# A two-layer decoder trunk on one core: a fixed TensorE order, another head grouping in layer A, and a softmax per token tile in layer B

## The chip, the cores and the metric

The kernel runs on one core of a Trainium2 chip. The metric is the device time of one execution in microseconds, the median of several runs. TensorE (PE in the profile) multiplies matrices; VectorE (DVE), ScalarE (ACT) and GpSimd (POOL) do the elementwise work, each taking its own queue in order; SyncE (SP) issues the DMAs.

## What is computed

A residual stream x of 256 tokens by 1024 goes through two layers in float32. Layer A is causal differential attention with 8 heads, each with two query/key pairs of width 64 and one value of width 128. Layer B is causal dilated sliding-window attention with 16 heads in each of three dilation groups. Each attention is followed by a squared-ReLU MLP of width 4096. Cut to what matters here:

```python
# layer A, per head h, components c = 0, 1
q, k, v = split(rms_norm(x, a_norm) @ w_qkv)       # q, k: RMS norm per 64, gain, rotary
p = softmax(mask(q @ k.T * 64 ** -0.5))            # for c = 0 and c = 1
o = (p[0] - lam * p[1]) @ v
x = x + rms_norm(o, sub_gain) * (1 - lam_init) @ w_o
x = x + square(relu(rms_norm(x) @ w_up)) @ w_down
# layer B: own q, shared k and v, groups (window, dilation) = (128,1), (512,4), (2048,16)
# per-head outputs of the groups are mixed by their softmax denominators: one softmax over all groups' keys
x = x + mix(softmax(mask(q @ k.T * 64 ** -0.5)) @ v) @ w_o
x = x + square(relu(rms_norm(x) @ w_up)) @ w_down
```

## The kernel before

Every float32 matrix product is made of three reduced-precision products: each operand is split into a high and a low part (high*high, high*low, low*high). For weights the class `Weights` does this: a chunk comes by DMA into one of three `raw` buffers (`fetch`, L69), ScalarE rounds half a chunk to `whi` (L82), VectorE subtracts to get `wlo` (L83); there are five buffers of each half. `W.pump` (L96) splits up to four halves ahead of the one in use.

Tokens lie in two tiles of 128 (t = 0, 1). `gemm` (L297) makes a projection of 384 columns in four weight halves; `gemm_half` (L283) issues 12 matmuls per half (2 token tiles x 2 contraction tiles x 3 products). After each half stands a call of `tick` (L211). In layer A a projection is one head: 128 columns of q, 128 of k, 128 of v. In layer B it is q, k or v of one head pair in all three groups, so three projections make one pair.

`qk_rows` (L310) turns the projected q and k of a token tile into normed, rotated rows: a square on ScalarE (L315), a multiplication by the rotary table on VectorE (`T`, L317), a sum (L321) and a scaling (L323) there, and three GpSimd operations (L328, L332, L334).

The attention of a head (or pair) is a Python generator, `attn_A` (L522) or `attn_B` (L596), whose stages are separated by `yield`; a yield of n is resumed n ticks later. The waits stand in `WAIT_A` and `WAIT_B` (L40, L41). The stages in layer A: transposes of q and k (`qk_T`, L352); scores (L350) with mask and row maximum on VectorE (`masked`, L368), then the negated and scaled maximum `nm` (L538), four exponentials on ScalarE (L541), and the combination of the two softmaxes (L545 to L550); transposes of the probabilities (L554); products with v (L565, L566) and the norm of the output (L569 to L580); transposes of the output (L584) and its split into `oh`, `ol`. In layer B: `qk_T` three times; scores of token tile 0 and 1 with their masks (L609); then one softmax stage over both tiles (L612 to L623: `nm`, exponentials, reciprocal, scaling); per head of the pair transposes (L632) and products with v (L646); at the end the split into `oh`, `ol` (L652).

PSUM has 8 banks in one ring (tag "bank"). A projection takes two, the output projection (`OutProj`, L390) four until its end, `qk_T` one, a pair of scores two, a group of transposes or products one.

After the last projection the output projection runs for heads 0 to 5, with a tick after each half of a head, and `finish` (L227) ticks until the head in question is done; the last two heads are added in `boundary` (L372) together with the start of the next stage. The instructions of each engine are put in order at compile time by a scheduler that goes by priorities and its own estimate of times; TensorE's too.

```python
WAIT_A = (2, 2, 4, 2, 3)
WAIT_B = (2, 2, 2, 2, 2, 3)
    for kt in range(KT - 2):
        finish(gens[kt])
        op.body(kt)
    for kt in range(KT - 2, KT):
        finish(gens[kt])
```

## Time and profile before

| what | value |
|---|---|
| median of 3 runs | 802.08 us (801.34 to 802.3) |
| the profiled execution | 801.55 us, its span 799.5 us |
| TensorE busy | 772.1 us (97%), 4408 matmuls |
| VectorE busy | 581.1 us (73%) |
| ScalarE busy | 467.0 us (58%) |
| GpSimd busy | 190.9 us (24%) |
| mean granted TensorE clock | 0.995 |
| layer A, first projection to first MLP matmul | 10.64 to 137.12 us |
| MLP of layer A | 137.12 to 317.65 us |
| layer B, first projection to first MLP matmul | 317.65 to 616.68 us |
| MLP of layer B | 616.68 us to the end |

Matmuls are pipelined, so a row's duration is longer than the time until the next may start; the distance between the starts of neighbouring rows is what one costs in a stream. The idle time in brackets at a row's end is counted from the modelled end of the matmul before it, so it is a little shorter than the time that was lost.

### The profile page before, as it was taken

What the parts mean: (1) busy time and instruction counts of PE and PEld (TensorE: products, weight loads), DVE (VectorE), ACT (ScalarE), POOL (GpSimd) and SP (SyncE); (2) the same over time, 40 slices, a digit from 0 to 9 for tenths busy, and PEclk for the clock granted to TensorE, in tenths of its full rate; (3) what the DMA queues carried; (4) which work ended last, traced back from release to release, by engine and by line L of the source; (5) the groups of instructions that cost most, each with busy time, mean ns of one, the idle gap of its engine ahead of it and who ended that gap; (6) DMA issues with size and microseconds to landing.
All of it is one profiled execution on the core that took longest, in us unless ns stands there. A gap on an engine that the chain in (4) does not pass through costs nothing.

```text
span 799.5 us, 11766 instructions
## 1 busy us (share of the span) xinstructions
PE 772.1 (97%) x4408; PEld 686.7 (86%) x4408; DVE 581.1 (73%) x985; ACT 467.0 (58%) x851; POOL 190.9 (24%) x191
## 2 busy tenths in 40 slices
PE   6999989999999999999999999999997999999998
PEld 6898967888888888999999999999886888888886
DVE  3998987666656666998888888888767666556663
ACT  5667777544444445657586674857766544444441
POOL 2553531300000000555336354363611000000000
PEclk9999999999999999999999999999999999999999
DMA  8643445445555542554443434434442455545531
GB/s 300 229 143 123 158 155 164 169 171 197 198 176 207 171 184 90 187 198 154 136 153 113 157 121 157 158 119 172 159 158 106 158 186 182 210 170 199 187 130 52
DMA packets 22328, 131.12 MB, mean 164 GB/s; under 512 B 2560, under 2 KB 3328, under 8 KB 13056
## 3 DMA queue, kind: packets, MB, share of 16 engines
q1 hardware_dynamic: 22272, 130.38, 46.0%
q8 instruction: 34, 0.56, 0.3%
q14 instruction: 22, 0.18, 0.1%
HBM read 129.32 MB, written 1.05 MB: 163 GB/s over the span
## 4 chain that ended last, share of the span: by engine, by line
PE 64%; DVE 17%; ACT 12%; issue 3%; POOL 2%; DMA 1%; SPq 0%; POOLq 0%; DVEq 0%; ACTq 0%
PE wps L435 15%; PE wps L437 7%; PE acc L488 7%; PE acc L489 7%; PE acc L490 7%; DVE wlo L83 5%; PE acc L292 4%; PE acc L294 4%; PE acc L293 4%; ACT whi L82 4%; ACT sm L618 2%; DVE sm L369 2%; PE wps L632 2%; DVE T L317 2%; ACT smA L541 2%
## 5 line engine op out<-in xcount | busy, mean ns | idle before, releaser
L83 DVE TENSOR_TENSOR wlo<-raw,whi 128x1024 fp32r<-128x1024 f32 (+1 forms) x272 | 307.0, 1138 | 153.9 <-ACT whi L82 153.7
L82 ACT ACTIVATE whi<-raw 128x1024 fp32r<-128x1024 f32 (+1 forms) x272 | 258.9, 957 | 211.1 <-issue 74.9
L435 PE MATMUL wps<-hT,whi 128*128 128x512 f32 x512 | 182.2, 399 | 2.0 <-DVE hT L271 2.0
L437 PE MATMUL wps<-hT,wlo 128*128 128x256 f32 x512 | 142.9, 280 | 0.0
L435 PEld LDWEIGHTS wps<-hT,whi 128*128 128x128 f32 x512 | 95.9, 188 | 26.0 <-DVE hT L271 3.2
L328 POOL TENSOR_TENSOR T<-T 128x384 f32<-128x384 f32 (+1 forms) x48 | 44.4, 924 | 280.5 <-DVE ms L243 181.6
L488 PE MATMUL acc<-whi,u 128*128 128x512 f32 x256 | 100.4, 392 | 0.3 <-ACT u L340 0.3
L489 PE MATMUL acc<-wlo,u 128*128 128x512 f32 x256 | 100.0, 391 | 0.0
L490 PE MATMUL acc<-whi,u 128*128 128x512 f32 x256 | 98.9, 389 | 0.0
L437 PEld LDWEIGHTS wps<-hT,wlo 128*128 128x128 f32 x512 | 96.6, 189 | 1.4
L292 PE MATMUL acc<-whi,hT 128*128 128x384 f32 x256 | 88.8, 349 | 0.3 <-ACT whi L82 0.2
L292 PE MATMUL acc<-whi,hK 128*128 128x384 f32 x256 | 87.6, 343 | 0.0
L293 PE MATMUL acc<-wlo,hT 128*128 128x384 f32 x256 | 86.3, 337 | 1.1 <-DVE wlo L83 1.1
L294 PE MATMUL acc<-whi,hT 128*128 128x384 f32 x256 | 86.2, 337 | 0.0
L294 PE MATMUL acc<-whi,hK 128*128 128x384 f32 x256 | 85.8, 335 | 0.0
L293 PE MATMUL acc<-wlo,hK 128*128 128x384 f32 x256 | 85.7, 335 | 0.0
L332 POOL TENSOR_TENSOR f<-ms,half 128x6 f32<-128x6 f32 (+1 forms) x48 | 68.2, 1422 | 4.6 <-DVE ms L323 3.1
L488 PEld LDWEIGHTS acc<-whi,u 128*128 128x128 f32 x256 | 48.1, 188 | 11.7 <-ACT u L340 1.2
L490 PEld LDWEIGHTS acc<-whi,u 128*128 128x128 f32 x256 | 48.1, 188 | 10.6 <-DVE u L341 0.4
L489 PEld LDWEIGHTS acc<-wlo,u 128*128 128x128 f32 x256 | 48.1, 188 | 8.8
L293 PEld LDWEIGHTS acc<-wlo,hT 128*128 128x128 f32 x256 | 48.6, 190 | 1.4 <-DVE wlo L83 1.4
L292 PEld LDWEIGHTS acc<-whi,hT 128*128 128x128 f32 x256 | 48.6, 190 | 1.4 <-ACT whi L82 0.5
(117 smaller groups left out, 1204.9 us busy)
## 6 DMA issues: line engine op xcount, KB each, us to landing
raw<-in_wB SPq DMA_DIRECT2D x48, 768.0 KB, 4.2
raw<-in_wup SPq DMA_DIRECT2D x32, 1024.0 KB, 4.8
raw<-in_wdn SPq DMA_DIRECT2D x32, 1024.0 KB, 4.8
raw<-in_wA SPq DMA_DIRECT2D x15, 768.0 KB, 4.3
raw<-in_woA SPq DMA_DIRECT2D x4, 1024.0 KB, 4.8
raw<-in_woB SPq DMA_DIRECT2D x4, 1024.0 KB, 4.8
early<-in_x SPq DMA_DIRECT2D x2, 512.0 KB, 5.3
x<-in_xp SPq DMA_DIRECT2D x1, 1024.0 KB, 7.5
```

Of the source, the lines that this page charges most:

```text
L82: self.nc.scalar.activation(hi[:, :n], raw, AF.Copy)
L83: self.nc.vector.tensor_tensor(lo[:, :n], raw, hi[:, :n].bitcast(F32), op=ALU.subtract)
L292: nc.tensor.matmul(ps, h[:, kt, 0, tok], wh[:, c], start=kt == 0, stop=False)
L293: nc.tensor.matmul(ps, h[:, kt, 0, tok], wl[:, c], start=False, stop=False)
L294: nc.tensor.matmul(ps, h[:, kt, 1, tok], wh[:, c], start=False, stop=kt == KT - 1)
L328: nc.gpsimd.tensor_tensor(u[:, :n].rearrange("p (h a d) -> p h a d", a=2, d=HD // 2), T[:, 0, :n].rearrange("p (h a d) -> p h a d", a=2, d ...
L332: nc.gpsimd.tensor_tensor(f[:, :nsub], ms[:, :nsub], half[:, :nsub], op=ALU.pow)
L435: nc.tensor.matmul(o, wh[:, c], self.h[:, kt].rearrange("p l s -> p (l s)"), start=kt == 0, stop=False, skip_group_check=True)
L437: nc.tensor.matmul(o[:, 0:S], wl[:, c], self.h[:, kt, 0, :], start=False, stop=kt == KT - 1, skip_group_check=True)
L488: nc.tensor.matmul(ps, uh[:, tok], dh[:, c], start=first, stop=False)
L489: nc.tensor.matmul(ps, uh[:, tok], dl[:, c], start=False, stop=False)
L490: nc.tensor.matmul(ps, ul[:, tok], dh[:, c], start=False, stop=last)
```

## The change

TensorE's instructions keep the order of the source: `tc.manual_schedule` takes that engine away from the scheduler. The other engines' orders are still made by it.

Layer A's projections are regrouped. A "qk" unit projects q and k of two heads (512 columns, four weight halves of two contraction tiles), a "v" unit the values of two heads (256 columns, two weight halves of four contraction tiles), in the order `UNITS`. A tick now also stands between the two token tiles of a half. The waits `WAIT_A` are longer in ticks, and the odd head of a unit waits three more. `qk_rows` handles both heads at once up to L332 and writes the product `T` into a part of the buffer `early`.

In both layers `masked` yields the negated, scaled minimum `nm` directly, with the scores scaled along, so the separate `nm` operation is gone. In layer A two more small VectorE operations go: one to ScalarE (a square), one to GpSimd (an addition of 128x2). In layer B the softmax is made per token tile, right after that tile's scores, and the projections of the last two pairs are reordered (`PAIRS`); a pair's attention starts after its k projection, with a longer wait.

```diff
-WAIT_A = (2, 2, 4, 2, 3)
-WAIT_B = (2, 2, 2, 2, 2, 3)
+WAIT_A = (7, 3, 6, 3, 5)
+WAIT_B = (4, 2, 2, 5, 2, 3)
+UNITS = [("qk", 0), ("qk", 1), ("v", 0), ("qk", 2), ("v", 1), ("qk", 3), ("v", 2), ("v", 3)]
+PAIRS = [(hp, i) for hp in range(HP - 2) for i in range(3)]
+PAIRS += [(HP - 2 + e, i) for e, i in ((0, 0), (0, 1), (1, 0), (1, 1), (0, 2), (1, 2))]
...
+    def gemm_A(h, key, n, nk):
+        pss = [accum() for _ in range(NT)]
+        for half in range(KT // nk):
+            gemm_half(pss, h, key, half // 2, half % 2, n, nk, tick)
+            if half < KT // nk - 1:
+                tick()
+        return pss
...
-        qn = wk.tile([P, 384], F32, name="qn", tag="qn", bufs=6)
-        nc.gpsimd.tensor_tensor(
-            qn[:, :n].rearrange("p (h d) -> p h d", d=HD), u[:, :n].rearrange("p (h d) -> p h d", d=HD),
-            f[:, :nsub, None].to_broadcast([P, nsub, HD]), op=ALU.mult)
+        for e in range(heads):
+            qn = wk.tile([P, 384], F32, name="qn", tag="qn", bufs=6)
+            nc.gpsimd.tensor_tensor(
+                qn[:, :n].rearrange("p (h d) -> p h d", d=HD),
+                u[:, e * n:(e + 1) * n].rearrange("p (h d) -> p h d", d=HD),
+                f[:, e * nsub:(e + 1) * nsub, None].to_broadcast([P, nsub, HD]), op=ALU.mult)
+            rows.append(qn)
...
-    def masked(out, ps, m, init, mx):
-        nc.vector.tensor_tensor_reduce(out, ps, m, 1.0, init, ALU.add, ALU.max, mx)
+    def masked(out, ps, m, nm):
+        nc.vector.tensor_tensor_reduce(out, ps, m, -(HD ** -0.5), 3e38, ALU.add, ALU.min, nm)
...
-        yield WAIT_A[0]
+        yield WAIT_A[0] + 3 * (hd % 2)
...
-        nm = small.tile([P, 4], F32, name="nm", tag="nm")
-        nc.vector.tensor_scalar(nm, mx, -(HD ** -0.5), None, op0=ALU.mult)
...
-        nc.vector.scalar_tensor_tensor(cf[:, :, 1], den[:, :, 0], EPS, den[:, :, 0], op0=ALU.mult, op1=ALU.mult)
+        nc.scalar.activation(cf[:, :, 1], den[:, :, 0], AF.Square, scale=EPS ** 0.5)
...
-        nc.vector.scalar_tensor_tensor(ms[:, :2], oss, 1.0 / P, cf[:, :, 1], op0=ALU.mult, op1=ALU.add)
+        nc.gpsimd.tensor_tensor(ms[:, :2], oss, cf[:, :, 1], op=ALU.add)
...
+            nm = small.tile([P, 2], F32, name="nm", tag="nm")
             for hh in range(2):
                 masked(sms[hh][:, b, :], scs[hh], mask[:, 4 * b:4 * b + 4, :].rearrange("p b k -> p (b k)"),
-                       -3e38, mxs[hh][:, b:b + 1])
-            yield WAIT_B[2 + b]
-        for hh in range(2):
-            sm = sms[hh]
+                       nm[:, hh:hh + 1])
             den = small.tile([P, 2], F32, name="den", tag="den")
-            nm = small.tile([P, 2], F32, name="nm", tag="nm")
-            nc.vector.tensor_scalar(nm, mxs[hh], -(HD ** -0.5), None, op0=ALU.mult)
-            for b in range(2):
-                nc.scalar.activation(sm[:, b, :], sm[:, b, :], AF.Exp, bias=nm[:, b:b + 1], scale=HD ** -0.5,
-                                     accum_out=den[:, b:b + 1])
+            for hh in range(2):
+                nc.scalar.activation(sms[hh][:, b, :], sms[hh][:, b, :], AF.Exp, bias=nm[:, hh:hh + 1],
+                                     scale=-1.0, accum_out=den[:, hh:hh + 1])
             rd = small.tile([P, 2], F32, name="rd", tag="rd")
             nc.vector.reciprocal(rd, den)
-            for b in range(2):
-                nc.scalar.activation(sm[:, b, :], sm[:, b, :], AF.Copy, scale=rd[:, b:b + 1])
-        yield WAIT_B[2]
+            for hh in range(2):
+                nc.scalar.activation(sms[hh][:, b, :], sms[hh][:, b, :], AF.Copy, scale=rd[:, hh:hh + 1])
+            yield WAIT_B[2 + b]
...
+    for kind, u in UNITS:
+        if kind == "qk":
+            pss = gemm_A(h, ("qk", u), 512, 2)
...
+            for t in range(NT):
+                tab = tabA[:, t].rearrange("p c g d -> p c (g d)")[:, :, None, :].to_broadcast([P, 2, 2, 4 * HD])
+                rows.append(qk_rows(pss[t], 8, ra[NT + t], tab, TA[t], 2))
+            tick()
+            for e in range(2):
+                qns = [rows[t][e] for t in range(NT)]
+                gens.append(start(attn_A(2 * u + e, qns, qns, vts[u], oh, ol)))
...
+        else:
+            pss = gemm_A(h, ("v", u), 256, 4)
+            for t in range(NT):
+                vt = wk.tile([P, 2, 2, P], F32R, name="v", tag="v", bufs=3)
...
+    for hp, i in PAIRS:
+        hx = hk if i else hq
+        pss = acc0 if hp == 0 and i == 0 else gemm(hx, ("B", hp, i), 384)
...
+        if i == 1:
+            gens.append(start(attn_B(hp, *[[rows[hp, e, t] for t in range(NT)] for e in range(2)], vts[hp],
+                                     oh, ol)))
...
-    with tile.TileContext(nc) as tc:
+    with tile.TileContext(nc) as tc, tc.manual_schedule(engines={mybir.EngineType.PE}):
```

## Rows read from the trace of the kernel before

**Rows 1.** Busy time by stretch: length, each engine's busy us (instructions), clock, DMA share, GB/s.
```profile
core 0: us, PE busy (x) PEld busy (x) DVE busy (x) ACT busy (x) POOL busy (x), PEclk, DMA share, GB/s
72.43:96.67 24.24, 22.33 (x151) 21.58 (x151) 22.08 (x65) 18.75 (x55) 10.63 (x14) 1.00 0.47 164
101.52:137.12 35.60, 31.51 (x161) 24.03 (x161) 28.51 (x73) 26.71 (x76) 7.70 (x10) 0.95 0.40 137
137.12:317.65 180.53, 180.20 (x912) 152.06 (x913) 113.91 (x143) 88.36 (x131) 8.29 (x12) 1.00 0.49 177
317.65:616.68 299.03, 291.01 (x1873) 273.86 (x1871) 244.31 (x416) 200.31 (x353) 131.10 (x113) 0.99 0.43 151
```
**Rows 2.** TensorE in layer A: start us, us, what; idle before it and releaser.
```profile
22.52 0.44 PE L293 MATMUL acc<-wlo,hT 128*128 128x384 f32 x1 [1.08 <-DVE wlo L83]
...
77.74 0.49 PE L554 MATMUL wps<-ident,smA 128*128 128x128 f32 x3
79.19 0.38 PE L350 MATMUL wps<-th,tl 64*128 64x256 f32 x2 [0.96 <-DVE tl L341]
```
**Rows 3.** Who waited for whom on TensorE: total us, times, longest.
```profile
PE wps L350 <- DVE tl L341: 4.1, 4, 1.9
```
**Rows 4.** ScalarE, layer A, the stretch before the scores at 79.19.
```profile
73.84 0.51 ACT L541 ACTIVATE smA<-smA,nm 128x256 f32<-128x256 f32 x1 [2.67 <-DVE nm L538]
...
77.11 0.58 ACT L340 ACTIVATE th<-wps 128x512 fp32r<-128x512 f32 x1
```
**Rows 5.** VectorE, the same stretch and the next.
```profile
72.42 1.31 DVE L83 TENSOR_TENSOR wlo<-raw,whi 128x768 fp32r<-128x768 f32 x1
73.65 0.15 DVE L538 TENSOR_SCALAR nm<-mx 128x4 f32<-128x4 f32 x1
...
78.46 0.68 DVE L341 TENSOR_TENSOR tl<-wps,th 128x512 fp32r<-128x512 f32 x1
...
81.59 0.95 DVE L83 TENSOR_TENSOR wlo<-raw,whi 128x768 fp32r<-128x768 f32 x1
```
**Rows 6.** GpSimd, two operations beside those weight splits.
```profile
72.30 0.61 POOL L334 TENSOR_TENSOR qn<-T,f 128x256 f32<-128x256 f32 x1
...
81.51 1.02 POOL L332 TENSOR_TENSOR f<-ms,half 128x4 f32<-128x4 f32 x1
```
**Rows 7.** VectorE by line and form: count, busy us, mean ns, idle before.
```profile
L317 DVE TENSOR_TENSOR T<-acc,tabB 128x768 f32<-128x768 f32 x32 | 30.3, 947 | 0.8 <-POOL qn L334 0.8
...
L317 DVE TENSOR_TENSOR T<-acc,tabA 128x512 f32<-128x512 f32 x16 | 10.9, 680 | 4.1 <-ACT sq L315 4.1
```
**Rows 8.** TensorE in layer A's tail: last head's products with v, then its transposes.
```profile
126.65 0.28 PE L566 MATMUL wps<-v,pA 128*128 128x256 f32 x1
126.77 0.40 PE L403 MATMUL acc<-wlo,oTh 128*128 128x512 f32 x1
127.00 0.40 PE L404 MATMUL acc<-whi,oTl 128*128 128x512 f32 x1
...
130.07 0.33 PE L584 MATMUL wps<-ident,orow 128*128 128x128 f32 x1 [0.18 <-ACT orow L580]
```
**Rows 9.** TensorE in layer B, a pair's first probability transposes.
```profile
403.33 0.33 PE L293 MATMUL acc<-wlo,hK 128*128 128x384 f32 x1
403.50 0.34 PE L294 MATMUL acc<-whi,hK 128*128 128x384 f32 x1
404.40 1.27 PE L632 MATMUL wps<-ident,sm 128*128 128x128 f32 x8 [0.56 <-ACT sm L623]
```
**Rows 10.** TensorE in layer B's tail.
```profile
606.92 1.22 PE L646 MATMUL wps<-p,v 128*128 128x512 f32 x6 [0.94 <-DVE p L341]
610.78 0.53 PE L402 MATMUL acc<-whi,oTh 128*128 128x512 f32 x1 [2.65 <-ACT oTh L340]
611.12 0.63 PE L403 MATMUL acc<-wlo,oTh 128*128 128x512 f32 x1
611.54 0.63 PE L404 MATMUL acc<-whi,oTl 128*128 128x512 f32 x1
```

More of the change, by code (lines that the diff above doesn't have):

```diff
@@ L130, in plan_mlp @@
                 plan(("dn", layer, j - 1), a["wdn"][layer, j - 1], 2 * DM)
-    for hd in range(KT):
-        for i in range(2):
-            plan(("A", hd, i), a["wA"][hd, i], 4 * 384)
+    for kind, u in UNITS:
+        for i in range(2 if kind == "qk" else 1):
+            plan((kind, u, i), a["w" + kind][u, i], WSLOT)
     for i in range(4):
@@ L137, in trunk @@
     plan_mlp(0)
-    for hp in range(HP):
-        for i in range(3):
-            for j in range(2):
-                plan(("B", hp, i, j), a["wB"][hp, i, j], 4 * 384)
+    for hp, i in PAIRS:
+        for j in range(2):
+            plan(("B", hp, i, j), a["wB"][hp, i, j], 4 * 384)
     for i in range(4):
@@ L281, in h_tile, with gemm_half @@
         return hpool.tile([P, KT, 2, S], F32R, name=tag, tag=tag)
-    def gemm_half(pss, h, key, j, i, n):
+    def gemm_half(pss, h, key, j, i, n, nk=2, between=None):
         wh, wl = W.get(at[(*key, j)], i)
         for t in range(NT):
+            if t and between:
+                between()
             tok = slice(t * P, (t + 1) * P)
             ps = pss[t][:, :n]
-            for k in range(2):
-                kt = 4 * j + 2 * i + k
+            for k in range(nk):
+                kt = nk * (2 * j + i) + k
                 c = slice(k * n, (k + 1) * n)
@@ L332, in qk_rows @@
         nc.gpsimd.tensor_tensor(f[:, :nsub], ms[:, :nsub], half[:, :nsub], op=ALU.pow)
[L333 to L337 removed]
+        rows = []
+        n, nsub = n // heads, nsub // heads
+        for e in range(heads):
[5 more added lines that the diff above has]
+            rows.append(qn)
+        return rows
     def split(out_hi, out_lo, ps):
@@ L519, in add, with attn_A @@
             nc.vector.scalar_tensor_tensor(xs, self.acc[t][n], self.rr[t], xs, op0=ALU.mult, op1=ALU.add)
-    def attn_A(hd, qr, kr, vt, oh, ol):
-        yield WAIT_A[0]
+    def attn_A(hd, qr, kr, vts, oh, ol):
+        yield WAIT_A[0] + 3 * (hd % 2)
         T = qk_T(qr, kr, (0, P))
         yield WAIT_A[1]
-        mx = small.tile([P, 4], F32, name="mx", tag="mx")
+        nm = small.tile([P, 4], F32, name="nm", tag="nm")
         den = small.tile([P, 2, 2], F32, name="den", tag="den")
@@ L564, in attn_A @@
                 b = j if q else 2
-                nc.tensor.matmul(o2, ph[:, b], vt[:, j], start=j == 0, stop=False)
-                nc.tensor.matmul(o2, pl[:, b], vt[:, j], start=False, stop=j == q)
+                vt = vts[j][:, hd % 2].rearrange("p l d -> p (l d)")
+                nc.tensor.matmul(o2, ph[:, b], vt, start=j == 0, stop=False)
+                nc.tensor.matmul(o2, pl[:, b], vt, start=False, stop=j == q)
         pov = po.rearrange("p (q l d) -> p q l d", q=2, l=2)
@@ L599, in attn_B @@
         yield WAIT_B[1]
-        mxs = [small.tile([P, 2], F32, name="mx", tag="mx") for _ in range(2)]
         sms = [wk.tile([P, 2, 4 * P], F32, name="sm", tag="sm") for _ in range(2)]
@@ L718, in trunk @@
     gens = []
-    for hp in range(HP):
-        rows = [[None] * NT, [None] * NT]
-        vts = []
-        for i, hx in ((0, hq), (1, hk), (2, hk)):
-            pss = acc0 if hp == 0 and i == 0 else gemm(hx, ("B", hp, i), 384)
-            for t in range(NT):
-                ps = pss[t]
-                if i < 2:
-                    rows[i][t] = qk_rows(ps, 2 * G, rb[NT + t], windows(tabB[:, i, t]))
-                else:
-                    vt = wk.tile([P, 2 * G, 2, HD], F32R, name="v", tag="v", bufs=3)
-                    psv = ps[:, :384].rearrange("p (g d) -> p g d", d=HD)
-                    nc.scalar.activation(vt[:, :, 0, :], psv, AF.Copy, scale=rb[t])
-                    nc.vector.scalar_tensor_tensor(vt[:, :, 1, :], psv, rb[t], vt[:, :, 0, :].bitcast(F32),
-                                                   op0=ALU.mult, op1=ALU.subtract)
-                    vts.append(vt)
-            tick()
-        gens.append(start(attn_B(hp, rows[0], rows[1], vts, oh, ol)))
+    rows, vts = {}, [[] for _ in range(HP)]
+    for hp, i in PAIRS:
+        hx = hk if i else hq
+        pss = acc0 if hp == 0 and i == 0 else gemm(hx, ("B", hp, i), 384)
+        for t in range(NT):
+            ps = pss[t]
+            if i < 2:
+                rows[hp, i, t] = qk_rows(ps, 2 * G, rb[NT + t], windows(tabB[:, i, t]))[0]
+            else:
+                vt = wk.tile([P, 2 * G, 2, HD], F32R, name="v", tag="v", bufs=3)
+                psv = ps[:, :384].rearrange("p (g d) -> p g d", d=HD)
+                nc.scalar.activation(vt[:, :, 0, :], psv, AF.Copy, scale=rb[t])
+                nc.vector.scalar_tensor_tensor(vt[:, :, 1, :], psv, rb[t], vt[:, :, 0, :].bitcast(F32),
+                                               op0=ALU.mult, op1=ALU.subtract)
+                vts[hp].append(vt)
+        tick()
+        if i == 1:
+            gens.append(start(attn_B(hp, *[[rows[hp, e, t] for t in range(NT)] for e in range(2)], vts[hp],
+                                     oh, ol)))
     op = OutProj("oB", oh, ol)
```

49 lines of the change are left out of this document (25 added, 24 removed).

## The prediction, made before the changed kernel ran

> **What bounds the kernel now.** I read the busy times by stretch first [rows 1]. In the MLP that follows layer A TensorE is busy for 180.20 of 180.53 us: nothing waits there, and the change doesn't touch it. What can be won lies in the two attention stretches. In a steady stretch of two heads of layer A, TensorE stands idle for 24.24 - 22.33 = 1.91 us, and VectorE is busy for 22.08 of the 24.24: TensorE is nearly, and VectorE almost as nearly, the bound. In layer B the idle time is 299.03 - 291.01 = 8.0 us of 299. So the prize is small: some 10 us in each layer.
>
> Then I asked which wait ends last. In layer A the scores of a head start at 79.19, 1.45 us after three small transposes began, and wait for `tl` [rows 2]; four such waits make 4.1 us [rows 3]. Why is `tl` late? It stands on VectorE at 78.46 [rows 5] because its other half `th` runs on ScalarE only at 77.11, and ScalarE had stood for 2.67 us in front of the exponentials of the head before, waiting for `nm` [rows 4]. `nm` itself takes 0.15, but stands behind a weight split of 1.31 us [rows 5]. One small operation, queued badly on VectorE, holds up ScalarE's queue and through it TensorE. In layer B the wait is another: a pair's first probability transposes wait for the scaling on ScalarE, 404.40 after 403.50 where 0.17 is a 384-column matmul's place in the stream [rows 9], so 0.73 lost (the bracket says 0.56: a wait costs about 0.17 more than its bracket). There are six of these. Both layers end in a tail in which TensorE runs out of work: in layer A 35.60 - 31.51 = 4.1 us idle at a mean clock of 0.95 [rows 1], in layer B idle times of 0.94 and 2.65 [rows 10].
>
> **The change, part by part.** *The projections.* Two heads had 2 x 48 matmuls of 384 columns; they get 48 of 512 and 48 of 256, the same columns. The rows give 0.23 for 512 and 0.12 for 256 [rows 8] against 0.17 for 384 [rows 9]; rounded to 10 ns this allows -1 to +2 us for the layer. I take 0.
>
> *VectorE in layer A.* A form's fixed share follows from two sizes of `T`: 947 - 680 = 267 ns for 256 more elements, so 680 - 2 x 267 = 146 ns per instruction [rows 7]. Per two heads go two weight splits, two `T`, two sums, two scalings, two value subtractions (all merged into larger ones), two `nm`, and two each of the small operations handed to ScalarE and GpSimd: 16 instructions, 16 x 0.146 = 2.3 us. VectorE falls from 22.1 to about 19.8 us per two heads, TensorE's own work stays near 22.3: VectorE no longer sets the pace. And `nm` leaves the chain: 1.31 + 0.15 us earlier exponentials [rows 5], more than the 0.96 that the scores wait [rows 2]. The longer `WAIT_A` is less than it seems: a tick was 12 x 0.17 = 2.1 us, it becomes 6 x 0.23 or 12 x 0.12 = 1.4 us. From `qk_T` to the scores 3 x 1.4 stand in place of 2 x 2.1, from the scores to the transposes 6 x 1.4 in place of 4 x 2.1: no more slack at the places that stall; the gain must come from the shorter chain. Only the first step (7 or 10 ticks for 2) and the last are longer. Removed: 4.1 + 4 x 0.17 = 4.8 us, and the wait of 1.08 (1.25) for the first weights of the second projection [rows 2], since a unit of eight steps gives its weights longer. What may stay or come new (the larger `T` operations in one burst, two more accumulators in the ring): 0 to 4.8; I take 1.0, near the lower end, because VectorE has 2.5 us in each 22 to spare.
>
> *The start.* The first half chunk grows from 384 to 512 KB ahead of x's second half on SP's queue. 128 KB at the 177 GB/s of a quiet stretch [rows 1] is 0.74, an upper bound; 0 if the queue is not full; I take 0.4.
>
> *Layer A's tail.* Here the fixed order costs something. I counted ticks by the source. The last q/k unit starts its heads at tick 40 of the 48 projection ticks; head 7's transposes of probabilities fall on tick 60, its product with v on 63, its output on 68. The twelve steps of the output projection last from tick 48 to 60. So behind the last of them TensorE has, in this order, v of head 6, transposes of head 7, v of head 7, outputs of 6 and 7, and only then the closing 24 matmuls. Nothing may be drawn forward into the gaps, as the scheduler did before: between the last product with v and the first output transposes stand matmuls of the output projection from 126.77 on [rows 8]. Uncovered are the split of the probabilities (0.94 + 0.17 for the like wait of layer B [rows 10]), and 130.07 - 126.77 = 3.3 from v to the output [rows 8], plus the addition moved to GpSimd: between 0 (it replaces one of VectorE's) and 0.9 (1.02 for four elements there [rows 6], less 0.15); I take 0.3. Sum 4.7. After an idle time of 2.65 the matmuls run at 611.54 - 611.12 = 0.42 instead of 0.23 [rows 10], nine of them there, the lower clock level: 9 x 0.19 = 1.7, which I expect again. The tail of before goes: 4.1 idle less the 1.9 counted among the four [rows 3], 2.2, and the clock's 1.8 (0.95 over 35.6 us is 3.6 us at half speed [rows 1]).
>
> Layer A: -4.8 - 1.25 - 2.2 - 1.8 + 1.0 + 0.4 + 4.7 + 1.7 = -2.2 us.
>
> *Layer B.* Token tile 0's half of the softmax starts with its own scores, two ticks ahead of tile 1's, and five ticks (10.4 us) instead of four lie between the last scores and the transposes. The instructions are the same. The six waits go: 6 x 0.73 = 4.4. The tail: pair 7 now starts at tick 88 of 96, its last product with v comes on tick 107 of the 108 that the output steps reach, so a step (6 x 0.23 = 1.4) and three closing matmuls (0.7) stand behind it, against a chain of 2.65 + 0.17 [rows 10]: 0.7 is left, and no drop of the clock. Removed: 0.94 + 2.65 + 2 x 0.17 = 3.9 and 1.7. New: around tick 96 the four banks of the output projection meet scores of pair 7 that can't be masked until pair 6's buffers are free; 0 to 3, I take 1.0, for VectorE has the time. `qk_T`, which wants three banks, comes one tick after the second transposes instead of two: 0 (the splits are done) to 1 per pair; I take 0.5 in all. Layer B: -4.4 - 5.6 + 0.7 + 1.5 = -7.8 us.
>
> Sum: -10.0 on the profiled execution's 801.55, **791.5 us**. The median, 802.08, lies 0.5 above it; I leave that in the range.
>
> **A rule of the skill against the trace.** Of the two weight splits in rows 5, the one that starts at 72.42 takes 1.31 beside a GpSimd multiplication of 0.61; the one at 81.59 takes 0.95 beside a GpSimd `f` of 1.02 [rows 5, 6]. The Trainium skill, "SBUF — State Buffer", section "SBUF: two separate sides", says that a VectorE operation with two SBUF inputs and a GpSimd operation that reads SBUF share a port pair as an exclusive lock, held for the whole instruction. By that rule the first is explained and the second should have waited about as long as `f` ran; the trace has no such wait. What it would mean here is the third rival.
>
> **The rivals.** (1) *VectorE's relief doesn't reach the chain*: the four waits stay (ordered anew, `th` still stands behind exponentials), the tails as above. Then layer A is 3.8 worse: 795.3. For it: the slack is not longer. Against: `nm`'s 1.46 us. 0.10. (2) *The fixed order blocks on PSUM banks*, the slower case. In layer B `qk_T`'s three banks come 2.1 us behind two transposes' banks and one of the products; VectorE empties them at 0.68 each [rows 5] between weight splits of 0.95 to 1.31. If it comes late with them, the engine's whole queue stands. Three operations and two splits are 4 to 4.7 us against the 2.1: 2 to 2.6 per pair, seven pairs, 2.5 x 7 = 17.5 - 0.5: 808.5. It makes the kernel slower from (10 + 0.5) / 7 = 1.5 us per pair on. For it: eight banks are counted full there. Against: before, the same banks are emptied beside the same work, and no wait of `qk_T` stands out. 0.13. (3) *The longer GpSimd operations hold up weight splits.* `f` now has eight elements: from 1.02 for four about 2.0, eight times in layer A; a split that waited for each would add up to 16 us of VectorE, of which four times 2.5 is spare: 6 us, 797.5. Against: the split at 81.59. 0.04. (4) *The order is no change*: TensorE already ran in this order in the steady stretches, so only the tails differ, and the waits move elsewhere: -5.6 + 2.2 in layer B, +2.4 in A's tail: within 1.5 of 801. 0.06.
>
> **How the numbers follow.** Forecast 0.67; the rivals 0.10, 0.13, 0.04, 0.06. Downward: no remaining waits (-1.0), no bank waits (-1.5), no clock drop in A's tail (-1.7), projections -1, start -0.4: 786. Upward: rivals 1 and 3 (798) and the upper bounds of the unknown costs in part; with 0.13 for the slower case and part of rival 4 outside, the range is 785.5 to 800. A difference under 0.2% (1.6 us) can't be told from none: faster 0.82, same 0.06, slower 0.12.
>
> **What would show it.** Right: in layer A no wait of the scores for `tl` and VectorE at 88 to 90% of a two-head stretch; an idle time of some 3 us before the last output transposes and a lower clock behind it; in layer B no wait of the transposes for ScalarE, under 1 us at the end. Wrong: waits of `qk_T` or of a first projection matmul for VectorE or ScalarE that repeat with each pair or unit (rival 2), weight splits over 2 us (rival 3), or matmuls of 512 and 256 columns that cost more than their columns.

## The result

The changed kernel takes 848.37 us (median of 4 runs, 847.74 to 848.68) against 802.19 before (4 runs, 801.34 to 802.56): a ratio of 1.0576, 95% interval 1.0558 to 1.0595. It is slower by 46 us, where 10 us less were forecast. Its profiled execution took 847.74 with a span of 846.0.

First the busy time by stretch of the changed kernel (layer A from its first projection, MLP, layer B, second MLP; columns as in [rows 1]).

```profile
10.51:149.90 139.39, 123.61 (x706) 104.34 (x705) 102.50 (x218) 86.39 (x226) 53.04 (x53) 0.93 0.42 155
149.90:337.40 187.50, 183.87 (x914) 153.27 (x913) 116.24 (x145) 89.71 (x130) 11.22 (x12) 0.99 0.48 172
337.40:658.90 321.50, 299.54 (x1873) 282.62 (x1872) 248.21 (x399) 198.51 (x353) 133.74 (x113) 0.96 0.39 137
658.90:846.00 187.10, 181.18 (x905) 151.16 (x904) 112.67 (x140) 84.43 (x117) 0.00 (x0) 1.00 0.46 163
```

Before, cut in the same way, layer A took 126.48 (TensorE busy for 118.11), the second MLP 182.82; the other two stand in [rows 1].

So +12.9 in layer A, +7.0 and +4.3 in the MLPs, +22.5 in layer B. TensorE does the same matmuls. Part of the loss is idle time (layer A: 139.39 - 123.61 = 15.8 against 8.4; layer B: 321.50 - 299.54 = 22.0 against 8.0), part is matmuls that take longer (123.61 against 118.11; 299.54 against 291.01) at a lower mean clock (0.93 against 0.99; 0.96 against 0.99). No stretch was spared. The longest waits of TensorE, over the whole execution (who waited <- for whom: us in all, times, longest):

```profile
PE wps L663 <- DVE p L362: 17.3, 6, 3.3
...
PE wps L606 <- ACT orow L602: 5.7, 3, 2.3
PE wps L378 <- POOL qn L353: 3.5, 1, 3.5
PE acc L510 <- ACT u L361: 3.1, 2, 2.2
PE wps L587 <- DVE pA L362: 2.8, 3, 1.1
...
PE wps L378 <- DVE v L707: 1.9, 1, 1.9
...
PE wps L371 <- DVE tl L362: 0.6, 2, 0.4
```

The last line answers to [rows 3]: the wait for `tl` fell from 4.1 to 0.6 (0.4 of it in layer A), as forecast. The six waits of the probability transposes for ScalarE's `sm` [rows 9] have no line any more. But longer waits came in other places. In layer B it is now the product with v (pv for short) that waits for the split `p` of the probabilities, in six of the eight pairs. TensorE, in one of them:

```profile
432.40 2.07 PE L663 MATMUL wps<-p,v 128*128 128x512 f32 x6 [3.27 <-DVE p L362]
```

and VectorE in the same stretch:

```profile
427.88 1.40 DVE L89 TENSOR_TENSOR wlo<-raw,whi 128x768 fp32r<-128x768 f32 x1
...
429.34 1.81 DVE L89 TENSOR_TENSOR wlo<-raw,whi 128x768 fp32r<-128x768 f32 x2
431.07 1.27 DVE L362 TENSOR_TENSOR p<-wps,p 128x512 fp32r<-128x512 f32 x2
```

Three weight splits stand ahead of `p`, with small operations of the q/k rows between them, and the six pv matmuls behind the wait take 2.07 instead of 1.20 (at 409.68 in the kernel before).

### The profile page after: what moved, and what is told of

Same layout as the page of the kernel before. It is cut to its first block, busy times and chain, and to the rows that moved or that the text cites. A ratio compares the mean times of both kernels' runs of the same rounds, so it can differ in the third digit from the quotient of the medians.

```text
span 846.0 us, 11613 instructions
## 1 busy us (share of the span) xinstructions
PE 791.8 (94%) x4408; PEld 694.6 (82%) x4408; DVE 582.7 (69%) x905; ACT 465.5 (55%) x835; POOL 198.3 (23%) x183
## 4 chain that ended last, share of the span: by engine, by line
PE 68%; DVE 15%; ACT 9%; issue 3%; POOL 3%; DMA 1%; SPq 0%; DVEq 0%; ACTq 0%; POOLq 0%
PE wps L457 14%; PE wps L459 7%; PE acc L512 7%; PE acc L510 7%; PE acc L511 7%; DVE wlo L89 5%; PE acc L299 5%; PE acc L301 5%; PE acc L300 5%; ACT whi L88 3%; PE wps L663 2%; DVE T L333 2%; PE acc L426 2%; ACT sm L635 1%; PE acc L424 1%
## 5 line engine op out<-in xcount | busy, mean ns | idle before, releaser
L88 ACT ACTIVATE whi<-raw 128x1024 fp32r<-128x1024 f32 (+1 forms) x264 | 255.7, 980 | 222.8 <-issue 73.4
L510 PE MATMUL acc<-whi,u 128*128 128x512 f32 x256 | 101.8, 397 | 3.1 <-ACT u L361 3.1
L512 PE MATMUL acc<-whi,u 128*128 128x512 f32 x256 | 101.9, 398 | 0.4 <-DVE u L362 0.4
L344 POOL TENSOR_TENSOR T<-T 128x384 f32<-128x384 f32 x32 | 38.0, 1188 | 249.6 <-DVE ms L248 184.0
L299 PE MATMUL acc<-whi,hT 128*128 128x384 f32 (+2 forms) x256 | 91.3, 357 | 1.6 <-ACT hT L273 0.8
L301 PE MATMUL acc<-whi,hT 128*128 128x384 f32 (+2 forms) x256 | 87.6, 342 | 0.3 <-DVE hT L276 0.3
L300 PE MATMUL acc<-wlo,hT 128*128 128x384 f32 (+2 forms) x256 | 87.6, 342 | 0.0
L348 POOL TENSOR_TENSOR f<-ms,half 128x6 f32<-128x6 f32 (+1 forms) x40 | 65.9, 1649 | 3.3 <-PE wps L371 1.7
L512 PEld LDWEIGHTS acc<-whi,u 128*128 128x128 f32 x256 | 48.5, 189 | 12.9 <-DVE u L362 1.7
L299 PEld LDWEIGHTS acc<-whi,hT 128*128 128x128 f32 x256 | 50.1, 196 | 5.0 <-ACT hT L273 1.1
L301 PEld LDWEIGHTS acc<-whi,hT 128*128 128x128 f32 x256 | 49.8, 194 | 3.4 <-DVE hT L276 0.6
```

Of the source, the lines that this page charges most:

```text
L88: self.nc.scalar.activation(hi[:, :n], raw, AF.Copy)
L299: nc.tensor.matmul(ps, h[:, kt, 0, tok], wh[:, c], start=kt == 0, stop=False)
L300: nc.tensor.matmul(ps, h[:, kt, 0, tok], wl[:, c], start=False, stop=False)
L301: nc.tensor.matmul(ps, h[:, kt, 1, tok], wh[:, c], start=False, stop=kt == KT - 1)
L344: nc.gpsimd.tensor_tensor(u[:, :n].rearrange("p (h a d) -> p h a d", a=2, d=HD // 2), T[:, 0, :n].rearrange("p (h a d) -> p h a d", a=2, d ...
L348: nc.gpsimd.tensor_tensor(f[:, :nsub], ms[:, :nsub], half[:, :nsub], op=ALU.pow)
```

## The experiments

Two theories stood at the start: T1, the order fixed at TensorE makes the loss; T2, the regrouping of the two layers does. The stretches are those of the two tables above.

**The fixed order alone** (e1: kernel before plus one line):

```diff
-    with tile.TileContext(nc) as tc:
+    with tile.TileContext(nc) as tc, tc.manual_schedule(engines={mybir.EngineType.PE}):
```

> The kernel before with TensorE's order fixed to the source's and nothing else changed. Theory 1 (the fixed order itself costs, also in the MLPs, whose source the change did not touch: the MLP tail of after has a wait of 2.18 us for u and 4.2 us more than before over its last 36 matmuls): the two MLP stretches get about 7 and 4 us longer as in after, layer A's and B's tails some us longer: 815 to 825 us. Theory 2 (the new stages of layer B, and of layer A, are placed badly, the order is harmless): 802 to 804 us.

Measured: 812.36, ratio 1.0131 (1.0116 to 1.0146). Layer A 127.0 (+0.5), MLPs 184.9 (+4.3) and 185.3 (+2.4), layer B 302.2 (+3.2). Between the two: the order costs 10 us, a fifth of the loss, and most of it in the MLPs, which the forecast left out.

**The change without the fixed order** (e2):

```diff
-    with tile.TileContext(nc) as tc, tc.manual_schedule(engines={mybir.EngineType.PE}):
+    with tile.TileContext(nc) as tc:
```

> The changed kernel with TensorE given back to the scheduler; all else stays. Theory 1: the loss is gone, at most 800 us, MLP stretches of 180.5 and 183 us as before, and the waits of v's products for the split p in layer B (17.3 us in 6 on TensorE in after) gone or small. Theory 2: the MLP stretches are as before, but layer B keeps most of its 22 us and layer A most of its 13: 830 us or more.

Measured: 836.39, ratio 1.0432 (1.0416 to 1.0447). Layer A 136.6, MLPs 182.8 and 184.5, layer B 319.1. T2 holds for the larger part: both layers lose most of it without the fixed order.

**Layer A changed, layer B staged as before** (e3), no fixed order; softmax per pair again, a pair started after its v; of layer B's edits only the masks that give the negated minimum stay:

```diff
-WAIT_B = (4, 2, 2, 5, 2, 3)
+WAIT_B = (2, 2, 2, 2, 2, 3)
-PAIRS += [(HP - 2 + e, i) for e, i in ((0, 0), (0, 1), (1, 0), (1, 1), (0, 2), (1, 2))]
+PAIRS = [(hp, i) for hp in range(HP) for i in range(3)]
...
```

> Without the fixed order, layer A regrouped as in after, layer B staged as before (softmax over both tiles, old pairs and waits; only the mask operation gives the negated minimum directly). My step of the prediction (VectorE relieved, nm out of the chain): layer A's stretch 3 to 8 us shorter than 126.5 us, the whole about 793 to 798 us. Rival (the 512-column units come in bursts that delay the other splits): layer A 5 to 13 us longer, the whole 807 to 815 us.

Measured: 835.33, ratio 1.0417 (1.0401 to 1.0432). Layer A takes 137.0, inside the rival's range. For the whole neither expectation holds, since layer B still takes 318.4 (319.1 in e2): putting its stages back gives next to nothing. What was left in layer B, or what layer A does to it, had to be the cause.

**The change with layer B's stages at their old places** (e4: fixed order, softmax per token tile):

```diff
-WAIT_B = (4, 2, 2, 5, 2, 3)
+WAIT_B = (2, 2, 2, 4, 2, 3)
...
-        if i == 1:
+        if i == 2:
```

> The changed kernel, fixed order kept, softmax per token tile kept, but in layer B the pairs in plain order, a pair started after its v projection and the probability transposes at the tick where they stood before. If the place of the first transposes (beside the evacuation of the k projection) makes the wait of 3.3 us for the split p: those six waits go, layer B's 321.5 us become 300 to 305, the whole 827 to 832 us. If the softmax per tile or the fixed order makes it: layer B stays over 315 us, the whole over 840 us.

Measured: 864.44, ratio 1.0768 (1.0747 to 1.079); layer B 338.7, and pv waits for `p` 25.2 us in nine. So the new places of layer B's stages (longer steps, an earlier start, another order of the last pairs) are not what costs; together they hide some 17 us of it.

From the traces a new theory, T3. VectorE's instructions run in the order in which the program's scheduler put them. Without the small `nm` operation, so the theory, it puts one more weight split between the softmax and the split `p`. **The kernel before with nothing but this edit in layer B** (e5):

```diff
-            nc.vector.tensor_scalar(nm, mxs[hh], -(HD ** -0.5), None, op0=ALU.mult)
-                nc.scalar.activation(sm[:, b, :], sm[:, b, :], AF.Exp, bias=nm[:, b:b + 1], scale=HD ** -0.5,
+                nc.scalar.activation(sm[:, b, :], sm[:, b, :], AF.Exp, bias=nms[hh][:, b:b + 1], scale=-1.0,
```

> The kernel before with one edit: the masks of layer B give the negated minimum that the exponentials take, so the small op nm falls away (the form that the change uses); nothing else. Theory T3 (without the small op the order that the program's scheduler gives VectorE puts a third weight split ahead of the split p of the probabilities, so each pair's pv waits 2 to 3 us and the clock drops behind it): layer B as long as in e3_A_alone, 318 us against 299, the whole about 820. Rival (layer B's loss comes with the regrouped layer A, by another layout of SBUF or of the weight stream): layer B 297 to 299, the whole 800 to 802.

Measured: 818.53, ratio 1.0201 (1.0184 to 1.0218): 16 us more by the medians. In the profiled execution layer B takes 318.1 (+19.1) and layer A 1.2 more than before, the MLPs take the same. All that for two small operations fewer in a pair. VectorE at the second pair, first before, then with this edit:

```profile
397.55 0.68 DVE L369 CUSTOM_DVE_ANT_0 sm<-wps,mask 128x512 f32<-128x512 f32 x1
...
403.77 0.96 DVE L83 TENSOR_TENSOR wlo<-raw,whi 128x768 fp32r<-128x768 f32 x1 [0.36 <-ACT whi L82]
406.96 1.46 DVE L83 TENSOR_TENSOR wlo<-raw,whi 128x768 fp32r<-128x768 f32 x1 [2.23 <-ACT whi L82]
408.34 1.27 DVE L341 TENSOR_TENSOR p<-wps,p 128x512 fp32r<-128x512 f32 x2
```

```profile
398.50 1.83 DVE L83 TENSOR_TENSOR wlo<-raw,whi 128x768 fp32r<-128x768 f32 x2 [1.72 <-ACT whi L82]
400.24 0.68 DVE L373 CUSTOM_DVE_ANT_0 sm<-wps,mask 128x512 f32<-128x512 f32 x1
...
406.65 0.93 DVE L83 TENSOR_TENSOR wlo<-raw,whi 128x768 fp32r<-128x768 f32 x1
408.87 1.83 DVE L83 TENSOR_TENSOR wlo<-raw,whi 128x768 fp32r<-128x768 f32 x2 [1.29 <-ACT whi L82]
410.61 1.28 DVE L341 TENSOR_TENSOR p<-wps,p 128x512 fp32r<-128x512 f32 x2
```

Between the last reciprocal `rd` and `p` stand two weight splits before and three with the edit, and `p` starts at 410.61 instead of 408.34. TensorE wants pv at about 409.6 in both. Its row with the edit:

```profile
411.95 1.21 PE L647 MATMUL wps<-p,v 128*128 128x512 f32 x6 [2.19 <-DVE p L341]
```

The transposes' waits for `sm` are gone here too; what is saved there is lost several times over at pv (17.3 us in seven). TensorE's idle time in layer B is 318.12 - 297.54 = 20.6 against 8.0, and its busy time 6.5 longer, at a clock of 0.97.

The third split alone isn't the cause, though. ScalarE in the same stretch, first before, then with the edit:

```profile
393.25 1.78 ACT L82 ACTIVATE whi<-raw 128x768 fp32r<-128x768 f32 x2
...
398.96 0.72 ACT L618 ACTIVATE sm<-sm,nm 128x512 f32<-128x512 f32 x1 [1.83 <-DVE nm L616]
...
406.83 1.05 ACT L340 ACTIVATE p<-wps 128x512 fp32r<-128x512 f32 x2
```

```profile
396.21 0.73 ACT L619 ACTIVATE sm<-sm,nm 128x512 f32<-128x512 f32 x1 [1.97 <-DVE nm L373]
...
397.63 1.57 ACT L82 ACTIVATE whi<-raw 128x768 fp32r<-128x768 f32 x2
...
409.48 1.06 ACT L340 ACTIVATE p<-wps 128x512 fp32r<-128x512 f32 x2
```

VectorE's `p` needs ScalarE's rounded half of `p`. With the edit the first of these is done at 410.05, so with ScalarE as it is, the third split can account for no more than the 0.56 from there to 410.61, of 2.27 in all. The order on ScalarE has changed too. Before, all exponentials wait for `nm`, behind the masks of both token tiles. With the edit the first tile's need their own masks alone, and the scheduler put them ahead of two weight roundings (397.63 instead of 393.25). VectorE's splits of these halves wait for them, and the second tile's masks, behind the splits, start at 400.24 instead of 397.55. From there on the pair is late. GpSimd's order in layer B is the one before, and TensorE's too, but for one matmul.

**Layer A changed, layer B untouched** (e6), `nm` and its old masks included (no fixed order):

> Layer A as in the change, in the scheduler's own order; layer B and its order as in the kernel before, the old mask and the op nm included. T3: layer B back at 299 to 300, layer A as in e3_A_alone (137 against 126.5), MLPs together +2 to 3, the whole about 815. Rival (B's loss comes with the regroup): layer B 315 to 320, the whole 832 to 836.

Measured: 815.31, ratio 1.0163 (1.0148 to 1.0178); layer A 137.1, MLPs 181.5 and 183.1, layer B 300.1. These are the numbers expected under T3. Layer A leaves layer B alone; its own +10.6 remain.

**A small operation put back** (e9: e5 with these lines), with the negated masks kept:

```diff
+            nm = small.tile([P, 2], F32, name="nm", tag="nn")
+            nc.vector.tensor_scalar(nm, nms[hh], 1.0, None, op0=ALU.mult)
```

> e5_B_mask_only with a small VectorE op of the old op's size (a copy of nm) put between the masks of layer B and the exponentials; the negated masks stay. With it VectorE's order in layer B is that of the kernel before again (two weight splits ahead of the splits p, not three). T3: layer B back at 298 to 300 with the six waits of the transposes for ScalarE's sm (about 4 us) and none of pv for p above 1 us, the whole 800 to 803. Rival (the negated form of the masks is itself what costs): layer B stays at 315 to 318, the whole 816 to 820.

Measured: 804.56, ratio 1.0033 (1.0023 to 1.0043); layer B 299.1. Adding an operation that computes nothing wins back 14 us by the medians, and the whole 19 of layer B:

```profile
PE wps L635 <- ACT sm L626: 3.8, 6, 1.0
...
PE wps L649 <- DVE p L341: 0.9, 1, 0.9
```

The waits are those of the kernel before again, and in layer B the order of the instructions is that of the kernel before on all four engines. The whole is 1.6 above the expected range; the MLPs of this execution took 182.0 and 184.3 (more on that below).

**The order kept wrong, pv later** (e10: e5 with one number changed):

```diff
-WAIT_B = (2, 2, 2, 2, 2, 3)
+WAIT_B = (2, 2, 2, 2, 3, 2)
```

> e5_B_mask_only with WAIT_B (2, 2, 2, 2, 3, 2): the first pv of a pair is issued one quarter of a projection (12 matmuls of 0.173, 2.1 us) later; the third weight split still stands ahead of the splits p. T3: the waits of pv for p, 15.4 us in six, shrink by 2.1 each to under 4 in all, layer B 300 to 304, the whole 801 to 806. Rival (the loss is not in that wait but in VectorE's load or the clock whatever pv does): layer B 312 or more, the whole 813 or more.

Measured: 803.75, ratio 1.0021 (1.0008 to 1.0034); layer B 302.1, pv's waits for `p` 5.2 us in three (under 4 were expected), 5.0 of them in the last two pairs. One quarter of a projection between transposes and pv hides the late `p`. Together e5, e9 and e10 settle what costs in e5: not the form of the masks and not VectorE's load, but the order that the scheduler gives ScalarE and VectorE without `nm`, by which `p` comes late for pv. What each link of that order contributes was not tried.

For the changed kernel this is shown in part. Its pv waits for `p` as well, but there ScalarE's half of `p` is done at 427.62, 3.45 ahead of VectorE's `p` at 431.07 (0.56 in e5): VectorE's queue alone is late, with splits and q/k rows. No run puts an operation back into that kernel, so that the missing `nm` makes the order there too is not shown.

**Both moved**, meant to beat the kernel before (e11: e5 with a pair started one step earlier, transposes and pv a step more):

```diff
-WAIT_B = (2, 2, 2, 2, 2, 3)
+WAIT_B = (1, 2, 2, 3, 3, 2)
```

> e5_B_mask_only with WAIT_B (1, 2, 2, 3, 3, 2): a pair starts one step earlier, the transposes and pv each get a step more. A version meant to beat both: neither the six waits for sm (3.9 us in the kernel before) nor those for p should be left; by these rows layer B 294 to 297, the whole 797 to 800. Rival (a step more lengthens the tail of the last pair by as much, or the earlier start waits for qn): 801 to 804.

Measured: 809.99, ratio 1.01 (1.0085 to 1.0115); layer B 307.5, outside both expectations. pv still waits 6.1 for `p`, in seven. The q/k transposes of the next pair now stand right behind, and wait for VectorE's `ot`:

```profile
PE wps L357 <- DVE ot L651: 5.8, 5, 1.5
```

**Layer A: the small edits alone** (e7: kernel before plus negated masks, `cf` by ScalarE's Square, `ms` on GpSimd, in layer A):

> The kernel before with layer A's small edits alone: negated masks without nm, cf by ScalarE's Square, ms added on GpSimd; no regroup, no fixed order, layer B untouched. Theory (layer A's +10 us belong to the regroup into units of two heads, the small edits relieve VectorE as predicted): layer A 124 to 127, the whole 799 to 803. Rival (the small edits, above all ms on GpSimd ahead of ors, hold orow late): layer A 130 or more, the whole 806 or more.

Measured: 802.98, ratio 1.0011 (1.0002 to 1.002); layer A 127.7. VectorE's busy time in the layer falls from 108.76 to 104.19, and the waits for `tl` from 4.1 to 2.6, but others grow: no gain, no loss (layer A is 0.7 above the expected range; in e5 and e9, which leave it untouched, it took 127.6 and 125.5). The +10.6 come with the regrouping into units of two heads and its waits in ticks. A regrouping without the small edits was not tried.

Where? ScalarE and GpSimd in e6 around the first head's output (start, us, what, idle before it and releaser):

```profile
67.88 2.55 POOL L347 TENSOR_TENSOR f<-ms,half 128x8 f32<-128x8 f32 x1
70.52 1.71 POOL L352 TENSOR_TENSOR qn<-early,f 128x256 f32<-128x256 f32 x2
...
72.45 0.70 POOL L602 TENSOR_TENSOR ors<-ms,half 128x2 f32<-128x2 f32 x1
```

```profile
73.19 0.69 ACT L604 ACTIVATE orow<-orow,ors 128x128 f32<-128x128 f32 x2 [5.13 <-POOL ors L602]
73.78 0.49 ACT L563 ACTIVATE smA<-smA,nm 128x256 f32<-128x256 f32 x1
```

The scaling of `orow` waits 5.13 us for `ors`, which stands on GpSimd behind the burst of a two-head unit. Behind the scaling on ScalarE stand another head's exponentials; their masks were done at 70.0. VectorE then idles 4.49 for those exponentials, and the splits `pA`, the copies of v and the products come late in turn.

**GpSimd's burst shortened** (e8: e6 with the power of layer A's `f` made a multiplication, which leaves out the normalization of q and k; instruction order unchanged on all engines):

```diff
-        nc.gpsimd.tensor_tensor(f[:, :nsub], ms[:, :nsub], half[:, :nsub], op=ALU.pow)
+        nc.gpsimd.tensor_tensor(f[:, :nsub], ms[:, :nsub], half[:, :nsub], op=ALU.mult if heads == 2 else ALU.pow)
```

> As e6_A_regroup_B_untouched, with the power of f in layer A's q/k rows (8 elements, 1.6 to 2.6 us on GpSimd, twice a unit) replaced by a multiplication of the same operands, which leaves out the normalization of q and k; all four engines keep the same order of instructions. Theory (the GpSimd queue of a two-head unit holds qn and the attention's ms and ors late): layer A 4 us or more shorter than in e6, its waits for qn and orow smaller. Rival (the length of GpSimd's queue is covered; waits come from VectorE's and ScalarE's orders): layer A within 1 us of e6.

Measured: 810.72, ratio 1.0105 (1.008 to 1.0129): 4.6 less than e6 by the medians; in the profiled executions layer A is 134.7 against 137.1. The wait for `qn` falls from 3.2 to 1.6, that for `orow` from 4.1 to 3.5; those for `pA` stay. Layer A lies between theory (4 or more) and rival (within 1): the length of the burst counts, but ScalarE still waits 4.17 there.

**The scaling off ScalarE's queue** (e12: e6 with one GpSimd operation for two of ScalarE):

```diff
-        for q in range(2):
-            nc.scalar.activation(orow[:, q, :], orow[:, q, :], AF.Copy, scale=ors[:, q:q + 1])
+        nc.gpsimd.tensor_tensor(orow, orow, ors[:, :, None].to_broadcast([P, 2, P]), op=ALU.mult)
```

> e6_A_regroup_B_untouched with the scaling of orow in layer A (two ScalarE ops of 0.39 behind GpSimd's power ors) done on GpSimd in one op, so that ScalarE's queue no longer waits there for ors with the next head's exponentials behind it. Theory (ScalarE's in-order wait of 5.1 us for ors behind a two-head GpSimd burst holds the next head's exponentials and with them pA and pv): pA waits fall from 4.6 to under 2.5, the wait for orow itself stays at 4 or grows by up to 1.5, layer A 2 to 5 us shorter than in e6 (137.06). Rival (PE's waits for pA come from the weight splits ahead of them on VectorE and ScalarE): pA waits stay, layer A within 1 us of e6 or longer.

Measured: 805.33, ratio 1.0045 (1.0031 to 1.0058): 10 us less than e6, twice the expected. Layer A 128.0 (in an execution of 803.26, the fastest of ten). TensorE's waits in layer A, e6 and then this kernel:

```profile
PE wps L608 <- ACT orow L604: 4.1, 2, 2.3
PE wps L377 <- POOL qn L352: 3.2, 1, 3.2
PE wps L589 <- DVE pA L361: 2.8, 3, 1.1
...
PE wps L588 <- ACT pA L360: 1.8, 2, 1.0
```

```profile
PE wps L607 <- POOL orow L603: 4.7, 2, 2.7
...
PE wps L588 <- ACT pA L360: 0.8, 1, 0.8
PE wps L589 <- DVE pA L361: 0.7, 1, 0.7
```

`orow` itself is no earlier (4.7), and yet the layer is 9 us shorter: what cost was the queue behind it. 5.3 of the 9 are matmuls that take less time (busy 122.96 to 117.63, at a mean clock of 0.97 instead of 0.94), which I had not put into the expectation.

**The fixed order with the MLP's last products rearranged** (e14: e1 plus this in `Mlp.group`):

```diff
-            for i in range(2):
-                for f in range(2):
-                    self.down_mm(NFC - 2 + i, self.tail[i], f, t, n)
+            if (t, n) == (0, 0):
+                for tt, nn in ((0, 0), (1, 0), (0, 1), (1, 1)):
+                    for f in range(2):
+                        self.down_mm(NFC - 2, self.tail[0], f, tt, nn)
+            for f in range(2):
+                self.down_mm(NFC - 1, self.tail[1], f, t, n)
```

> e1_order_only (the kernel before with the fixed order: 812.4, MLP stages 184.9 and 185.3) with the last products of the MLP written in another order: the products of the last but one chunk of all four accumulators first, those of the last chunk, which need the newest u, behind them. Theory (the fixed order's loss in the MLPs is the wait of 2.2 us for u after six matmuls): that wait is gone at both MLPs' ends, MLP 0 182 to 183, MLP 1 182.5 to 183.5, the whole 807 to 809. Rival (the loss is in the transposes' wait for hT or in the clock): MLPs within 0.7 of e1's, the whole 811 or more.

Measured: 807.76, ratio 1.0072 (1.0056 to 1.0089); MLPs 182.1 and 183.9 (the second 0.4 above its range). In the source only six products of the chunk before stand ahead of those that need the last `u`; the scheduler had put others between. TensorE in the changed kernel:

```profile
324.82 0.51 PE L510 MATMUL acc<-whi,u 128*128 128x512 f32 x1 [2.18 <-ACT u L361]
...
326.80 0.63 PE L510 MATMUL acc<-whi,u 128*128 128x512 f32 x1
327.22 0.63 PE L511 MATMUL acc<-wlo,u 128*128 128x512 f32 x1
```

2.18 idle, then a matmul every 0.43 instead of 0.23, from 326.37 to 329.36. In e14 this wait is gone. What stays of e1's loss is the wait of the MLPs' first products for `hT` (2.3 in two), layer B's +3.3 and, in this execution, +2.1 in layer A.

**Cures together**, first without the fixed order (e13: e2 with the scaling on GpSimd and `WAIT_B = (4, 2, 2, 5, 3, 2)`), then the whole change with all three (e15):

> The whole change without its fixed order (e2_no_fixed_order: 836.4, layer A 136.6, layer B 319.1), with two cures and nothing undone: in layer A the scaling of orow on GpSimd (as in e12), in layer B the first pv one quarter of a projection later (WAIT_B (4, 2, 2, 5, 3, 2), as in e10). If the two causes are all of it: layer A 127 to 130, layer B 301 to 305, MLPs 181.5 and 183.5, the whole 804 to 810. Rival (softmax per token tile has a cost of its own in layer B): layer B 310 or more, the whole 814 or more.

> The change as it is (848.4: layer A 139.4, MLPs 187.5 and 187.0, layer B 321.5), fixed order kept, with the three cures of e12, e10 and e14. If the three causes add up: layer A 129 to 132, layer B 303 to 308, MLPs 183 to 185, the whole 812 to 819, which is what the fixed order costs e1 and little more. Rival (under the fixed order the waits move on to other places, as in a chain): above 825.

Measured: 815.74 (1.0177; 1.0147 to 1.0206) and 820.79 (1.0239; 1.0224 to 1.0254). Layer A 129.9 and 131.2, layer B 307.8 and 309.8, MLPs 182.8 and 184.6, 183.0 and 185.6. Three edits of a few lines take back 27.6 of the 46.2 us. The first kernel's whole falls to the rival's side (814 or more), its layer B between the two; the second is 2 us above its range. Layer B keeps 9 and 11 us, now spread over many waits (e13):

```profile
PE wps L662 <- DVE p L362: 4.4, 5, 0.9
PE wps L378 <- DVE ot L666: 4.3, 5, 1.0
```

So layer B's other edits (softmax per token tile, the places of its stages, the order of the last pairs) have a price of their own of about 6 (307.8 against 302.1 in e10; e13's profiled execution is 2.6 above its median). Which of them it comes from was not tried.

Also open: part of the MLPs' loss. Without the fixed order too, the MLPs of the kernels with the regrouped layer A are 0.2 to 2.4 us longer than before, with few waits to show for it. Some 1.4 of an MLP are not idle time: the 512-column matmuls start 0.233 apart on average instead of 0.231, all through it, in the changed kernel, e2, e3, e4, e13 and e15. They do so in e9 too, whose layer A is the old one, and not in e6, e8 and e12, so the regrouping by itself isn't the reason. No run shows what is. No kernel beat the one before.

## Why the prediction was wrong

*"Nothing waits there, and the change doesn't touch it"* (the MLP). This step failed: 11 us, priced at nothing. Nothing waited there [rows 1] because the scheduler had ordered it so; the fixed order holds for the whole kernel, and the rows of the stretch said nothing of what the source order would be. 6.8 of the 11 are the order's (e1); the rest is open. With it fell rival 4 (the order is no change, 0.06): alone it costs 10 us.

*The start, 0.4.* Nothing: the first projection starts at 10.51 instead of 10.64.

*Projections, 0.* Held: 512 columns start every 0.23, 256 every 0.12, the same columns at the same price.

*VectorE's relief in layer A.* The mechanism held, the conclusion did not. VectorE's busy time fell by 6.3 in the layer (108.76 to 102.50; 2.3 for each two heads, 9.2, were forecast), the waits for `tl` from 4.1 to 0.4, that for the first weights from 1.08 to nothing. Yet the layer became 12.9 longer, not 2.2 shorter.

*New waits in layer A: "0 to 4.8; I take 1.0".* This term was mis-sized, and its bound was no bound. Ahead of the tail the new waits are those for `qn` (3.50), `orow` (2.31), `pA` (0.97 and 1.11) and VectorE's `v` (1.91): 9.8 in brackets, and matmuls at the lower clock behind them. I looked at VectorE's load and at slack in ticks. The largest part came through two other queues: `ors` behind GpSimd's two-head burst, and exponentials behind it on ScalarE (e12: 9 us, 5.3 of them in matmuls that take less time). The forecast had the pattern in its own first section, one small operation badly queued holds ScalarE and through it TensorE, and asked it only of the operation that was removed. It did not ask it of what the larger units queue up. A second part is the first `qn`, 3.5 late, which had no term at all: GpSimd takes two heads of one tile before the first head of the other. No run tried a cure for it.

```profile
37.19 0.90 PE L378 MATMUL wps<-ident,qn 128*128 128x128 f32 x3 [3.50 <-POOL qn L353]
```

*Layer A's tail, +4.7 and +1.7.* Right in mechanism and size. TensorE of the changed kernel, answering to [rows 8]:

```profile
135.26 0.38 PE L586 MATMUL wps<-v,pA 128*128 128x256 f32 x1 [0.76 <-ACT pA L361]
136.34 0.38 PE L587 MATMUL wps<-v,pA 128*128 128x256 f32 x1 [0.69 <-DVE pA L362]
...
138.94 0.77 PE L606 MATMUL wps<-ident,orow 128*128 128x128 f32 x2 [1.75 <-ACT orow L602]
141.30 0.77 PE L606 MATMUL wps<-ident,orow 128*128 128x128 f32 x2 [1.59 <-ACT orow L602]
```

The brackets add up to 4.8, and from 142.30 to 145.28 the matmuls behind them start 0.43 apart, eight in all: 8 x 0.2 = 1.6.

*Layer B, -4.4 for the six waits, 0.7 left of the tail.* Both held: no wait for `sm`, and in the tail only 0.81 and 0.56 for `oTh` and `oTl`, with no drop of the clock (compare [rows 10]). *New in layer B, 1.0 and 0.5* failed: pv's waits for `p`, 17.3 in brackets, and 8.5 of slower matmuls. I wrote "The instructions are the same", and that was the error. They weren't, for `nm` was gone, and e5 and e9 show what such a removal does: it changes the order of those that stay, on two engines. The `p` split was just in time before (done at 409.62, pv at 409.68) and I never looked at it, because nothing waited for it.

*The rivals.* Rival 2 had the place (every pair of layer B, VectorE late behind weight splits) and the sign, but the wrong consumer: in layer B `qk_T` waited for VectorE nowhere (in layer A once, the 1.9 above), pv 17.3. Its 808.5 is far off too. Rival 3 was turned about (below): weight splits over 1.5 us are four of 34 in layer A, 2.5 us more in all, and none exceeds 2.0. Rival 1 did not happen: the waits for `tl` did go. The range of 785.5 to 800 left out everything above, because each case in it priced one wait, and none let the work behind a wait be queued in another order or, but for layer A's tail, slowed by the clock.

## What to carry to other kernels

On engines that run their instructions in order, ask of a change not only what it removes but which instruction will stand ahead of the next one that TensorE needs, on every engine; a lighter engine can be later. Look for the steps that are just in time without a wait, since those are where a shift of one operation shows. A fixed order counts for every stretch of the kernel, and its price is found where the schedule before differs from the source, also where nothing waited.

## What the runs showed of the hardware

A wait costs more than its bracket when the clock falls behind it, but not each does: pv took 2.07 behind 3.27 us of idle time at 432.40 in the changed kernel, where the granted clock was 0.50 from 432.2 to 435.5, and 1.21 behind 2.19 in e5, where it stayed at 1.00.

`f` on GpSimd has two durations. In the changed kernel:

```profile
29.30 2.64 POOL L348 TENSOR_TENSOR f<-ms,half 128x8 f32<-128x8 f32 x1
...
34.81 1.63 POOL L348 TENSOR_TENSOR f<-ms,half 128x8 f32<-128x8 f32 x1
```

with VectorE beside it:

```profile
28.47 1.95 DVE L89 TENSOR_TENSOR wlo<-raw,whi 128x1024 fp32r<-128x1024 f32 x1
30.48 3.90 DVE L89 TENSOR_TENSOR wlo<-raw,whi 128x1024 fp32r<-128x1024 f32 x3
```

No weight split runs beside the `f` at 34.81; where one is running as `f` starts, it takes 2.55 to 2.64 with eight elements. With six, in layer B, it is 1.32 or 2.05. And the split at 28.47 takes 1.95 instead of 1.21 where it begins in GpSimd's addition that runs from 28.04 to 29.34. This is the exclusive lock of the Trainium skill, "SBUF — State Buffer", section "SBUF: two separate sides": whichever starts first has the shared port pair for its whole instruction. These rows agree with it; only a split that begins while `f` runs is not held up ([rows 5, 6], the 0.95 beside an `f` of 1.02). The forecast took that one case for the rule's answer. Its price falls on GpSimd, whose burst grows by some 2.6 us ahead of the first head (2.64 for 1.63, and 2.83 for 1.18 of two `qn`), and so into the wait of 3.5 for `qn`.
